# Storing the seven summed quarters of an activation where it is made, moving weight and quarter sums from GpSimd to VectorE, and chaining two of the seven products in PSUM

## The chip, the core and the metric

The kernel runs as one program on one core of a Trainium2 chip. The metric is the device time of one execution in microseconds. In what follows PE is the matmul engine, DVE is VectorE, ACT is ScalarE, POOL is GpSimd, and SP is the engine whose queue issues most transfers.

## What is computed

The reference is a two-layer encoder trunk on 1024 tokens of 1024 features, all in fp32.

```
h = x                                             # [1, 1024, 1024]
z = gelu(rmsnorm(h) @ a_w_in)                     # 1024 -> 2 * 2048
u, v = split(z); v = layernorm(v)
sv = masked(w_s) @ v + b_s                        # by groups of 256 columns, blocks of 128 tokens
h = h + (u * sv) @ a_w_out                        # 2048 -> 1024
h = h + square(relu(rmsnorm(h) @ w1[0])) @ w2[0]  # 1024 -> 4096 -> 1024
kv = shared latent keys and values of rmsnorm(h)  # computed once
h = h + attention(q(rmsnorm(h)), kv) @ w_o        # 8 heads, causal by chunks of 64
h = h + square(relu(rmsnorm(h) @ w1[1])) @ w2[1]
return rmsnorm(h)
```

Nearly all of the arithmetic is in the large products: `a_w_in`, `a_w_out`, the two `w1`, the two `w2` and `w_o`.

## The kernel before

**Operands in two parts.** Every fp32 operand of a large product is cut into a high part (a cast on ACT, L181) and a low part (the difference, a subtraction on DVE, L182). A product of 128 columns by 512 tokens over 512 features is then 4 blocks of features times 3 passes, 12 matmuls of 512 columns (`prod`, L224). Weights are split a piece of 128x512 at a time into tiles `w` (six buffers); activations are split a quarter at a time into tiles `xq`.

**Seven products instead of eight.** A large product C = A.T @ B is cut in two along columns, features and tokens. With Winograd's form of Strassen's scheme seven products of quarters replace eight:

```
S1 = A21 + A22   S2 = S1 - A11   S3 = A11 - A21   S4 = A12 - S2
T1 = B12 - B11   T2 = B22 - T1   T3 = B22 - B12   T4 = B21 - T2
P1 = A11 B11  P2 = A12 B21  P3 = S4 B22  P4 = A22 T4  P5 = S1 T1  P6 = S2 T2  P7 = S3 T3
C11 = P1 + P2                C12 = P1 + P6 + P5 + P3
C21 = P1 + P6 + P7 + P4      C22 = P1 + P6 + P7 + P5
```

A is a weight matrix, B an activation. The S are called weight sums below and the T quarter sums.

**Up-projections** (`pair_block`). The seven quarters of B stay on chip (`Resident`). A block takes 256 columns of weights (two loads `wr` of 512 KB, into four buffers), makes the four weight sums on POOL (L280, L282, L283, L293), splits seven pieces and runs 7 x 12 = 84 matmuls, then joins four outputs of 128x512 in PSUM and SBUF and hands them on. There are 8 such blocks in the u half of the first mixer (each output is also multiplied by a gate, `gate`, and POOL multiplies the weights by the norm's gain, L435) and 16 in each of the two MLPs, of which the first two run side by side (`mlp`). The v half of the first mixer has tokens as rows and its own four sums of 128x1024 on POOL, four times. The finished activation block goes to DRAM scratch (`y_d`, `g_d`; `o_d` after the attention) as four stores of 256 KB.

**Down-projections** (`down`). The activation comes back from DRAM in chunks of 1024 features: 2 chunks for `a_w_out`, 4 for each `w2`, 1 for `w_o`, 11 in all. A chunk loads four quarters of B (8 loads `yr` of 512 KB) and eight pieces of weights (`wr`), makes four quarter sums on the way (`tsum`, L212: one half of each on DVE and one on POOL, 128x1024), four weight sums for each of four column blocks m on POOL (L696 to L700), splits 7 quarters and 28 weight pieces, and runs 28 x 12 = 336 matmuls. Products 1, 6, 7 and 4 accumulate in one PSUM bank for each m (`da`); products 2, 5 and 3 have their own (`dc`). Results are added into SBUF tiles `acc` by DVE (L659): eight additions for each m.

**Order.** The program does not write out the order on the engines: a scheduler decides it for each engine from dependences and buffers. Each engine then runs its own list strictly in order, and so does each queue of transfers.

## Time and profile before

| what | value |
|---|---|
| median of 3 executions | 2450.53 us (2447.11 to 2450.75) |
| the profiled execution: span from first to last instruction | 2453.1 us |
| PE busy | 2256.7 us (92% of the span) |
| DVE busy | 1946.0 us (79%) |
| ACT busy | 1107.0 us (45%) |
| POOL busy | 954.0 us (39%) |
| moved by DMA | 257.96 MB, mean 105 GB/s |
| chain of work that ended last | PE 58%, DVE 28%, issue 6%, DMA 5%, ACT 2%, POOL 1% |

The profiled execution is one execution of its own; its span is its whole time, with nothing shown around it. Busy time is summed over instructions, and PE's matmuls overlap one another in the records, so a busy PE is not a PE that starts a matmul as often as it can.

### The profile page before, as it was taken

How to read it: one execution, taken by the hardware profiler on the slowest of the kernel's cores; microseconds unless marked ns; L12 is line 12 of the kernel's file. 1: busy time of each engine (PE TensorE's matmuls, PEld its weight loads, DVE VectorE, ACT ScalarE, POOL GpSimd, SP SyncE). 2: the span in 40 equal slices, each digit the busy share in tenths (PEclk: the TensorE clock that was granted, in tenths of full speed). 3: DMA queues.
4: the chain of work that ended last, by engine and by line, in shares of the span. 5: the costliest groups of instructions: out<-in, count | busy, mean ns of one | idle time of the engine just before them, and what ended most of it. 6: DMA issues, size and time to landing. Idle time of an engine off the chain costs nothing.

```text
span 2453.1 us, 31584 instructions
## 1 busy us (share of the span) xinstructions
PE 2256.7 (92%) x11299; PEld 1919.9 (78%) x11299; DVE 1946.0 (79%) x3040; ACT 1107.0 (45%) x2124; POOL 954.0 (39%) x616
## 2 busy tenths in 40 slices
PE   6999888898899998988989999997999999889897
PEld 6998767677678887777879898886778888678776
DVE  8647989998975558899885777779985656988997
ACT  5443334335544444433355454553654444334345
POOL 5446445643633236335431103016432333454262
PEclk8999999999999999999999999998999999899999
DMA  5224334542243335421412101033134336324302
GB/s 204 93 91 133 107 108 125 189 137 79 72 138 105 118 114 199 138 86 52 137 48 72 30 27 34 31 134 129 69 106 139 108 108 217 109 75 137 112 26 69
DMA packets 173560, 257.96 MB, mean 105 GB/s; under 512 B 13566, under 2 KB 123227, under 8 KB 173403
## 3 DMA queue, kind: packets, MB, share of 16 engines
q1 hardware_dynamic: 164016, 239.12, 30.0%
...
## 4 chain that ended last, share of the span: by engine, by line
PE 58%; DVE 28%; issue 6%; DMA 5%; ACT 2%; POOL 1%; SPq 0%; ACTq 0%; DVEq 0%; POOLq 0%
PE a L224 12%; PE da L224 11%; DVE xq L182 8%; PE dc L224 6%; DVE w L182 6%; PE c L224 6%; PE va L471 4%; PE b L224 3%; PE sc L999 3%; PE lps L837 3%; DMA V<-v_d 2%; DVE yr L212 2%; DVE acc L659 2%; PE po L1046 2%; DVE V L562 1%
## 5 line engine op out<-in xcount | busy, mean ns | idle before, releaser
L224 PE MATMUL a<-xq,w 128*128 128x512 f32 x1920 | 468.5, 396 | 27.8 <-ACT o L287 15.5
L224 PE MATMUL da<-xq,w 128*128 128x512 f32 x2112 | 489.2, 391 | 4.8 <-DVE acc L659 3.7
L224 PEld LDWEIGHTS da<-xq,w 128*128 128x128 f32 x2112 | 397.6, 189 | 88.5 <-issue 4.5
L224 PE MATMUL dc<-xq,w 128*128 128x512 f32 x1536 | 385.4, 412 | 83.5 <-DVE acc L659 49.1
L224 PEld LDWEIGHTS a<-xq,w 128*128 128x128 f32 x1920 | 364.0, 191 | 106.2 <-ACT o L287 16.5
L224 PEld LDWEIGHTS dc<-xq,w 128*128 128x128 f32 x1536 | 306.8, 201 | 157.1 <-issue 63.2
L181 ACT CAST w<-wr 128x512 fp32r<-128x512 f32 x424 | 261.5, 620 | 332.7 <-PE da L224 187.8
L182 DVE TENSOR_TENSOR w<-wr,w 128x512 fp32r<-128x512 f32 x424 | 362.3, 855 | 43.4 <-ACT w L181 43.3
L182 DVE TENSOR_TENSOR xq<-yr,xq 128x512 fp32r<-128x512 f32 x308 | 286.1, 949 | 2.3 <-ACT xq L181 2.3
L181 ACT CAST xq<-yr 128x512 fp32r<-128x512 f32 x308 | 181.5, 619 | 201.6 <-DVE yr L212 61.3
L224 PE MATMUL c<-xq,w 128*128 128x512 f32 x960 | 238.2, 398 | 11.7 <-DVE o L309 6.6
L696 POOL TENSOR_TENSOR S<-wr,wr 128x512 f32<-128x512 f32 x44 | 66.1, 1520 | 453.6 <-DMA wr<-in_mlp_w_dram 250.4
L182 DVE TENSOR_TENSOR w<-S,w 128x512 fp32r<-128x512 f32 x164 | 169.1, 1032 | 79.6 <-ACT w L181 79.4
L224 PEld LDWEIGHTS c<-xq,w 128*128 128x128 f32 x960 | 183.3, 193 | 52.3 <-issue 8.2
L280 POOL TENSOR_TENSOR S<-wr,wr 128x512 f32<-128x512 f32 x40 | 58.0, 1449 | 347.8 <-DMA wr<-in_mlp_w_dram 298.5
L181 ACT CAST w<-S 128x512 fp32r<-128x512 f32 x164 | 100.4, 619 | 134.0 <-POOL S L293 95.0
L212 POOL TENSOR_TENSOR yr<-yr,yr 128x1024 f32<-128x1024 f32 x44 | 124.1, 2820 | 21.7 <-DVE xq L182 17.9
L733 POOL TENSOR_TENSOR ssq<-ssq,sq 128x512 f32<-128x512 f32 x52 | 77.7, 1495 | 138.4 <-ACT sq L732 138.1
L784 ACT ACTIVATE o<-o 128x512 f32<-128x512 f32 x96 | 60.6, 633 | 155.8 <-DVE o L783 155.8
L659 DVE TENSOR_TENSOR acc<-da,acc 128x512 f32<-128x512 f32 x144 | 98.1, 681 | 32.8 <-PE da L224 32.6
L224 PE MATMUL b<-xq,w 128*128 128x512 f32 x480 | 120.8, 390 | 0.0
L471 PE MATMUL va<-wv,xq 128*128 128x256 f32 x768 | 103.6, 296 | 12.2 <-DVE xq L182 7.3
...
## 6 DMA issues: line engine op xcount, KB each, us to landing
wr<-in_mlp_w_dram SPq DMA_DIRECT2D x128, 512.0 KB, 5.0
yr<-y_d SPq DMA_DIRECT2D x64, 512.0 KB, 4.3
...
wr<-in_a_w_in_dram SPq DMA_DIRECT2D x32, 512.0 KB, 5.6
acc<-h_d SPq DMA_DIRECT2D x32, 512.0 KB, 7.1
...
v_d<-V SPq DMA_DIRECT2D x16, 512.0 KB, 2.6
V<-v_d SPq DMA_DIRECT2D x16, 512.0 KB, 4.9
```

The source lines that it names most:

```text
L181: nc.scalar.copy(hi, src)
L182: eng.tensor_tensor(lo, src, hi.bitcast(F32), op=ALU.subtract)
L212: e.tensor_tensor(flat(x), flat(y), flat(z), op=op)
L224: mm = nc.tensor.matmul(o, lhsT=w[:, wi, p, :], rhs=xq[p][:, xi, :], start=first and p == 0 and ip == 0, stop=p == 3 and ip == 2, skip_gro ...
L280: nc.gpsimd.tensor_tensor(S1, A21, A22, op=ALU.add)
L471: nc.tensor.matmul(oo, lhsT=xq[p][:, xi, t * P:(t + 1) * P], rhs=w[wi][:, p, :], start=first and t % 2 == 0 and p == 0 and ip == 0, stop=p ...
L659: nc.vector.tensor_tensor(x, src, x, op=ALU.add)
L696: nc.gpsimd.tensor_tensor(S1, A21, A22, op=ALU.add)
L733: nc.gpsimd.tensor_tensor(ssq[:, sl], ssq[:, sl], sq, op=ALU.add)
L784: nc.scalar.activation(y, y, AF.Square)
L837: nc.tensor.matmul(o, lhsT=X2[k % 2, j][k // 2][:, xi, tt * P:(tt + 1) * P], rhs=self.wt[k][:, wi, :], start=k == 0 and ip == 0, stop=k == ...
L999: nc.tensor.matmul(sc[c][:, 0:n], lhsT=lh, rhs=kk[c][:, part, 0:n], start=io == 0, stop=io == len(ops) - 1)
```

## The change

The activation blocks that go to DRAM are no longer the four raw quarters but the seven quarters that the products take. `Seven` takes over the scratch tensors; whoever makes a block calls `put`, which stores B11, B21 and B22 as they are and makes T1, T3, T2 and T4 (numbered by product: 5, 7, 6, 4) with one DVE subtraction of 128x512 each, as soon as their terms are there.

```diff
+    class Seven:
+        def store(self, n, f, t):
+            nc.sync.dma_start(self.d[f // 4, n - 1, f % 4 // 2][:, f % 2], t)
+        def put(self, f, i, j, t):
+            b = j ^ self.flip
+            B = self.got.setdefault(f, {})
+            B[i, b] = t
+            if (i, b) != (0, 1):
+                self.store({(0, 0): 1, (1, 0): 2, (1, 1): 3}[i, b], f, t)
+            def minus(n, x, y, into=None):
+                t = t2([P, 512], f"T{n}") if into is None else into
+                nc.vector.tensor_tensor(t, x, y, op=ALU.subtract)
+                self.store(n, f, t)
+                B[n] = t
+            if 5 not in B and (0, 0) in B and (0, 1) in B:
+                minus(5, B[0, 1], B[0, 0], B[0, 1] if 7 in B else None)
+            if 7 not in B and (0, 1) in B and (1, 1) in B:
+                minus(7, B[1, 1], B[0, 1], B[0, 1] if 5 in B else None)
+            if 6 not in B and 5 in B and 7 in B:
+                minus(6, B[1, 1], B[5], B[1, 1])
+            if 4 not in B and 6 in B and (1, 0) in B:
+                minus(4, B[1, 0], B[6])
...
-            nc.sync.dma_start(g_d[g // 4, m, j, g % 4 // 2][:, g % 2], u)
+            g_q.put(g, m, j, u)
```

`down` loads one quarter for each product, two products ahead, and makes no quarter sums. Its weight sums are on DVE. With the order 1, 2, 5, 3, 6, 7, 4 product 3 is added to product 5 in PSUM, after product 5 has been added to its other output.

```diff
-    def down(acc, y, nch, wsrc, hprev, hnext, after, order=(1, 2, 5, 6, 7, 4, 3), last=None, rpool=(None, "s"),
+    def down(acc, y, wsrc, hprev, hnext, after, order=(1, 2, 5, 3, 6, 7, 4), rpool=("s", None), last=None,
...
+            def piece(n, m):
+                A11, A21, A12, A22 = R[m, 0][:, :, lo], R[m, 0][:, :, hi], R[m, 1][:, :, lo], R[m, 1][:, :, hi]
                 if n == 5:
-                    tsum(B[0, 0], B[0, 1], B[0, 0], ALU.subtract, TENG)
...
-                        nc.gpsimd.tensor_tensor(S1, A21, A22, op=ALU.add)
-                        nc.gpsimd.tensor_tensor(A21, A11, A21, op=ALU.subtract)
-                        nc.gpsimd.tensor_tensor(A11, S1, A11, op=ALU.subtract)
-                    elif n == 3:
-                        nc.gpsimd.tensor_tensor(A12, A12, A11, op=ALU.subtract)
+                    nc.vector.tensor_tensor(S[m], A21, A22, op=ALU.add)
+                    w = w_piece(S[m])
+                    nc.vector.tensor_tensor(S[m], S[m], A11, op=ALU.subtract)
+                    return w
+                if n == 3:
+                    nc.vector.tensor_tensor(A21, A11, A21, op=ALU.subtract)
+                    nc.vector.tensor_tensor(A11, A12, S[m], op=ALU.subtract)
+                return w_piece({1: A11, 2: A12, 3: A11, 4: A22, 6: S.get(m), 7: A21}[n])
+            for at, n in enumerate(order):
+                xq = quarter(Q.pop(n))
+                if at + 2 < len(order):
+                    Q[order[at + 2]] = loadQ(order[at + 2])
...
+                    elif n == 3 and chained:
+                        o = c[m]
                     else:
-                        put(0, 1, m, o, True)
+                        o = c[m] = ps("dc")
+                    prod(o, w, xq, n in (1, 2, 5) or (n == 3 and not chained))
```

A quarter is split in two steps of 128x1024 instead of four of 128x512, the weight sums of the up-projections and of the v half move to DVE, and both halves of the resident quarter sums are on DVE.

```diff
     def quarter(raw):
-        for p in range(4):
-            x = slot([P, 2, 512], F32R, "xq")
-            split(x[:, 0], x[:, 1], raw[p // 2][:, p % 2])
-            q.append(x)
+        for r in raw:
+            x = [slot([P, 2, 512], F32R, "xq") for _ in range(2)]
+            split(flat(x[0]), flat(x[1]), flat(r))
+            q += [[part[:, p] for part in x] for p in range(2)]
...
     def pair_block(X, R, finish):
-        nc.gpsimd.tensor_tensor(S1, A21, A22, op=ALU.add)
+        nc.vector.tensor_tensor(S1, A21, A22, op=ALU.add)
...
-        nc.gpsimd.tensor_tensor(S2, S1, A11, op=ALU.subtract)
-        nc.gpsimd.tensor_tensor(A21, A11, A21, op=ALU.subtract)
+        nc.vector.tensor_tensor(S2, S1, A11, op=ALU.subtract)
+        nc.vector.tensor_tensor(A21, A11, A21, op=ALU.subtract)
...
-        nc.gpsimd.tensor_tensor(S2, A12, S2, op=ALU.subtract)
+        nc.vector.tensor_tensor(S2, A12, S2, op=ALU.subtract)
...
-                    tsum(T1, B[0, 1], B[0, 0], ALU.subtract, TENG)
+                    tsum(T1, B[0, 1], B[0, 0])
```

Besides, the first mixer takes the second half of the tokens first, `w_o` runs in the order 1, 5, 3, 6, 7, 2, 4, the stores after the attention move from ACT's queue to SP's, and comments are gone.

The lists of the engines show where the moved work stands. The first place is DVE's list in the second chunk of the first MLP's down-projection, before the change, around the quarter sums for products 6 and 7 (`yr`) and the first pieces of product 5 (`w`<-`S1`).

```order
L659 TENSOR_TENSOR acc1131_8095<-dc1293_9208,acc1131_8095 128x512
L182 TENSOR_TENSOR xq1335_9419<-yr1294_9222,xq1335_9419 128x512
L182 TENSOR_TENSOR w1328_9363<-wr1299_9232,w1328_9363 128x512
L182 TENSOR_TENSOR xq1336_9422<-yr1295_9224,xq1336_9422 128x512
L212 TENSOR_TENSOR yr1294_9222<-yr1320_9330,yr1294_9222 128x1024
L659 TENSOR_TENSOR acc1106_7990<-da1306_9246,acc1106_7990 128x512
L182 TENSOR_TENSOR w1330_9380<-wr1303_9240,w1330_9380 128x512
L212 TENSOR_TENSOR yr1300_9234<-yr1300_9234,yr1294_9222 128x1024
L659 TENSOR_TENSOR acc1106_7990<-da1307_9247,acc1106_7990 128x512
L182 TENSOR_TENSOR w1332_9397<-wr1305_9244,w1332_9397 128x512
L659 TENSOR_TENSOR acc1107_7991<-da1308_9248,acc1107_7991 128x512
L182 TENSOR_TENSOR w1339_9432<-S11338_9428,w1339_9432 128x512
```

The same list after the change, where the chunk before ends (`w`<-`wr1164` to `wr1167` are its last pieces, whose buffers `wr1264` to `wr1267` take over) and the second chunk's first weight sums stand.

```order
L182 TENSOR_TENSOR w1252_8610<-wr1164_8098,w1252_8610 128x512
L702 TENSOR_TENSOR acc1185_8191<-da1171_8109,acc1185_8191 128x512
L182 TENSOR_TENSOR xq1283_8779<-yr1262_8686,xq1282_8778 128x1024
L182 TENSOR_TENSOR w1253_8626<-wr1165_8100,w1253_8626 128x512
L182 TENSOR_TENSOR xq1285_8783<-yr1263_8688,xq1284_8782 128x1024
L702 TENSOR_TENSOR acc1182_8186<-da1168_8106,acc1182_8186 128x512
L182 TENSOR_TENSOR w1254_8642<-wr1166_8102,w1254_8642 128x512
L708 TENSOR_TENSOR S1302_8870<-wr1258_8678,wr1264_8690 128x512
L702 TENSOR_TENSOR acc1182_8186<-da1169_8107,acc1182_8186 128x512
L708 TENSOR_TENSOR S1305_8890<-wr1259_8680,wr1265_8692 128x512
L713 TENSOR_TENSOR wr1258_8678<-wr1258_8678 128x4x128
L182 TENSOR_TENSOR w1255_8658<-wr1167_8104,w1255_8658 128x512
```

The quarter sums are gone, a quarter's split is one row for two blocks, and the weight sums `S` stand between the splits and the additions, a few rows behind the split that frees the buffer of their weights.

The second place is DVE's list in the middle of an up-projection of the MLP, one block's worth of joins and splits, before the change.

```order
L309 TENSOR_TENSOR o11893_6310<-b900_6391,o11893_6310 128x512
L182 TENSOR_TENSOR w912_6463<-S1909_6444,w912_6463 128x512
L783 SCALAR_TENSOR_TENSOR o11893_6310<-o11893_6310,rbc536_4156 128x512
L182 TENSOR_TENSOR w914_6480<-S2910_6446,w914_6480 128x512
L300 TENSOR_TENSOR o12897_6345<-c889_6289,o12897_6345 128x512
L783 SCALAR_TENSOR_TENSOR o12897_6345<-o12897_6345,rbc536_4156 128x512
L182 TENSOR_TENSOR w916_6498<-S2910_6446,w916_6498 128x512
L182 TENSOR_TENSOR w917_6522<-wr904_6435,w917_6522 128x512
L304 TENSOR_TENSOR o22895_6327<-a888_6288,o22895_6327 128x512
L182 TENSOR_TENSOR w919_6544<-wr905_6437,w919_6544 128x512
L783 SCALAR_TENSOR_TENSOR o22895_6327<-o22895_6327,rbc536_4156 128x512
```

The same place after the change: `S1`<-`wr1114`, `wr1115` is the first weight sum of a block whose first product is a whole block away; `T7`, `o12` (5) and `o22` (6) are quarter sums.

```order
L182 TENSOR_TENSOR w1110_7735<-wr1095_7633,w1110_7735 128x512
L303 TENSOR_TENSOR o221083_7525<-a1076_7486,o221083_7525 128x512
L182 TENSOR_TENSOR w1111_7758<-wr1095_7633,w1111_7758 128x512
L813 SCALAR_TENSOR_TENSOR o221083_7525<-o221083_7525,rbc552_4200 128x512
L348 TENSOR_TENSOR T71088_7582<-o221083_7525,o121085_7543 128x512
L182 TENSOR_TENSOR w1118_7786<-wr1114_7780,w1118_7786 128x512
L348 TENSOR_TENSOR o121085_7543<-o121085_7543,o111081_7508 128x512
L279 TENSOR_TENSOR S11139_7938<-wr1134_7929,wr1135_7931 128x512
L348 TENSOR_TENSOR o221083_7525<-o221083_7525,o121085_7543 128x512
L813 SCALAR_TENSOR_TENSOR y1092_7624<-a1076_7486,rbc552_4200 128x512
L281 TENSOR_TENSOR S21140_7940<-S11139_7938,wr1134_7929 128x512
L282 TENSOR_TENSOR wr1134_7929<-wr1134_7929 128x4x128
```

DVE has 22 instructions a block instead of 14: four weight sums and four quarter sums more. The two weights that `S1` takes are loaded into the buffers of `wr1074` and `wr1075`, and the row `w1091` is the last to read the second of them; five rows behind `S1` stands `w1102`, the low part of the next block's piece for product 5. PE takes that piece's high part in two matmuls right behind product 1, then runs the 12 matmuls of product 6 of the block before, and only then needs the low part.

The third place is POOL's list in the u half of the first mixer, before the change: one block's work.

```order
L435 TENSOR_TENSOR wr498_3924<-wr498_3924,gT_88 128x1024
L182 TENSOR_TENSOR vh454_3660<-V424_3456,vh454_3660 128x512
L435 TENSOR_TENSOR wr499_3927<-wr499_3927,gT_88 128x1024
L280 TENSOR_TENSOR S1505_3947<-wr498_3924,wr499_3927 128x512
L282 TENSOR_TENSOR S2506_3949<-S1505_3947,wr498_3924 128x512
L283 TENSOR_TENSOR wr498_3924<-wr498_3924 128x4x128
L293 TENSOR_TENSOR S2470_3719<-wr459_3683,S2470_3719 128x512
L182 TENSOR_TENSOR vh477_3789<-V465_3706,vh477_3789 128x512
L182 TENSOR_TENSOR vh482_3827<-V465_3706,vh482_3827 128x512
L182 TENSOR_TENSOR vh488_3866<-V464_3700,vh488_3866 128x512
L182 TENSOR_TENSOR vh494_3904<-V464_3700,vh494_3904 128x512
```

After the change POOL has only the gain's multiplications and the splits `vh` there, and the sums stand on DVE, as here around the first sum of the last u block (`S1519`).

```order
L625 SCALAR_TENSOR_TENSOR sv453_3602<-svp454_3603,gT_88,B2391_3217 128x256
L625 SCALAR_TENSOR_TENSOR sv453_3602<-svp455_3610,gT_88,B2391_3217 128x256
L279 TENSOR_TENSOR S1519_3982<-wr512_3959,wr513_3962 128x512
L628 SCALAR_TENSOR_TENSOR sv448_3565<-svp449_3566,gT_88,sv448_3565 128x256
L628 SCALAR_TENSOR_TENSOR sv448_3565<-svp450_3573,gT_88,sv448_3565 128x256
L182 TENSOR_TENSOR w480_3740<-wr470_3706,w480_3740 128x512
L628 SCALAR_TENSOR_TENSOR sv453_3602<-svp454_3603,gT_88,sv453_3602 128x256
L600 TENSOR_SCALAR V514_3965<-V514_3965,mv_2148,rstd_2157 128x256 x4
L628 SCALAR_TENSOR_TENSOR sv453_3602<-svp455_3610,gT_88,sv453_3602 128x256
L281 TENSOR_TENSOR S2520_3984<-S1519_3982,wr512_3959 128x512
L282 TENSOR_TENSOR wr512_3959<-wr512_3959 128x4x128
L299 TENSOR_TENSOR o12445_3542<-c437_3486,o12445_3542 128x512
```

The sum `S1519` stands in DVE's list between the steps of the gate (`sv`), and it needs both multiplications that POOL does after the loads.

## Rows read from the trace of the kernel before

**Rows 1.** Windows: length, each engine's busy us (instructions), granted clock, DMA share, GB/s.

```profile
core 0: us, PE busy (x) PEld busy (x) DVE busy (x) ACT busy (x) POOL busy (x), PEclk, DMA share, GB/s
785.52:804.56 19.04, 19.04 (x85) 15.77 (x85) 11.32 (x14) 8.03 (x14) 5.91 (x4) 1.00 0.36 111
...
331.00:361.50 30.50, 26.89 (x130) 21.73 (x130) 26.63 (x48) 9.52 (x18) 15.46 (x12) 1.00 0.35 108
...
1069.45:1155.55 86.10, 79.07 (x337) 64.92 (x337) 77.24 (x93) 32.75 (x56) 36.98 (x20) 0.96 0.30 98
...
425.00:622.00 197.00, 176.57 (x759) 144.40 (x758) 185.32 (x231) 90.80 (x162) 101.86 (x58) 0.94 0.40 136
945.00:1298.00 353.00, 322.68 (x1366) 264.55 (x1364) 316.98 (x378) 149.78 (x261) 158.20 (x88) 0.95 0.30 100
2080.00:2420.00 340.00, 310.68 (x1340) 253.84 (x1339) 306.57 (x364) 136.02 (x235) 151.21 (x82) 0.96 0.27 89
...
1650.00:1750.00 100.00, 84.96 (x391) 70.01 (x391) 94.28 (x126) 53.83 (x107) 48.18 (x29) 0.93 0.34 122
1750.00:1816.00 66.00, 57.44 (x255) 47.26 (x254) 62.97 (x87) 39.30 (x76) 37.12 (x21) 0.92 0.26 84
```

**Rows 2.** Waits in the chunk from 1069.45 to 1155.55: total us, times, longest.

```profile
PE dc L224 <- DVE acc L659: 13.4, 2, 7.0
```

**Rows 3.** Groups of DVE in the same chunk: count, busy us, mean ns, idle before.

```profile
L182 DVE TENSOR_TENSOR xq<-yr,xq 128x512 fp32r<-128x512 f32 x29 | 27.8, 976 | 0.0
L182 DVE TENSOR_TENSOR w<-wr,w 128x512 fp32r<-128x512 f32 x24 | 21.4, 890 | 0.0
L659 DVE TENSOR_TENSOR acc<-da,acc 128x512 f32<-128x512 f32 x16 | 10.9, 683 | 4.8 <-PE da L224 4.8
L659 DVE TENSOR_TENSOR acc<-dc,acc 128x512 f32<-128x512 f32 x16 | 10.5, 674 | 0.0
L212 DVE TENSOR_TENSOR yr<-yr,yr 128x1024 f32<-128x1024 f32 x4 | 6.8, 1702 | 4.1 <-DMA yr<-y_d 4.1
L182 DVE TENSOR_TENSOR w<-S,w 128x512 fp32r<-128x512 f32 x4 | 5.6, 1412 | 0.0
```

**Rows 4.** Groups of POOL in the same chunk.

```profile
L212 POOL TENSOR_TENSOR yr<-yr,yr 128x1024 f32<-128x1024 f32 x4 | 11.1, 2770 | 1.3 <-DVE xq L182 1.2
...
L696 POOL TENSOR_TENSOR S<-wr,wr 128x512 f32<-128x512 f32 x4 | 5.6, 1423 | 42.1 <-DMA wr<-in_mlp_w_dram 42.1
```

**Rows 5.** Groups of DVE in three up-projection blocks, 785.52 to 842.64.

```profile
L783 DVE SCALAR_TENSOR_TENSOR o<-o,rbc 128x512 f32<-128x512 f32 x9 | 9.4, 1049 | 0.0
L182 DVE TENSOR_TENSOR w<-S,w 128x512 fp32r<-128x512 f32 x9 | 9.3, 1028 | 8.9 <-ACT w L181 8.9
L182 DVE TENSOR_TENSOR w<-wr,w 128x512 fp32r<-128x512 f32 x12 | 8.3, 690 | 4.4 <-ACT w L181 4.4
```

**Rows 6.** Waits in the same three blocks.

```profile
POOL S L280 <- DMA wr<-in_mlp_w_dram: 35.6, 3, 12.2
```

**Rows 7.** The page's DMA issues: count, KB each, median us from issue to landing.

```profile
wr<-in_mlp_w_dram SPq DMA_DIRECT2D x128, 512.0 KB, 5.0
yr<-y_d SPq DMA_DIRECT2D x64, 512.0 KB, 4.3
...
wr<-in_a_w_in_dram SPq DMA_DIRECT2D x32, 512.0 KB, 5.6
acc<-h_d SPq DMA_DIRECT2D x32, 512.0 KB, 7.1
```

**Rows 8.** Groups of DVE in two u blocks, 331.00 to 391.60.

```profile
L562 DVE TENSOR_SCALAR V<-V,mv,rstd 128x256 f32<-128x256 f32 x18 | 15.3, 888 | 8.4 <-DMA V<-v_d 8.4
L590 DVE TENSOR_TENSOR o<-o,sv 128x512 f32<-128x512 f32 x6 | 7.3, 1220 | 0.0
...
L586 DVE SCALAR_TENSOR_TENSOR sv<-svp,gT,B 128x256 f32<-128x256 f32 x16 | 7.0, 468 | 0.0
```

**Rows 9.** Groups of POOL in the same two u blocks.

```profile
L435 POOL TENSOR_TENSOR wr<-wr,gT 128x1024 f32<-128x1024 f32 x5 | 9.5, 1897 | 27.7 <-DMA wr<-in_a_w_in_dram 15.8 <-DVE w L182 7.7 <-DVE sv L586 4.3
...
L280 POOL TENSOR_TENSOR S<-wr,wr 128x512 f32<-128x512 f32 x3 | 4.9, 1646 | 0.2
```

More of the change, by code (lines that the diff above doesn't have):

```diff
@@ L137, in trunk_kernel @@
     xt = []
-    for t in range(4):
+    for t in range(4, NT):
         xx = slot([P, D], F32, "x")
@@ L324, in trunk_kernel, with __init__ @@
     h_d = [scratch(1, f"h_d{i}")[0] for i in range(4)]
-    y_d = [scratch(4, f"y_d{i}") for i in range(2)]
-    g_d = scratch(2, "g_d")
-    o_d = scratch(1, "o_d")
+    class Seven:
+        def __init__(self, nch, flip, name):
+            self.d = dpool.tile([nch, 7, 2, P, 2, 512], F32, name=name)
+            self.flip = flip
+            self.got = {}
+        def store(self, n, f, t):
[19 more added lines that the diff above has]
+                minus(4, B[1, 0], B[6])
+            if 4 in B:
+                del self.got[f]
+    y_q = [Seven(4, 1, f"y_d{i}") for i in range(2)]
+    g_q = Seven(2, 1, "g_d")
+    o_q = Seven(1, 1, "o_d")
     NF = DR // 2
@@ L443, in trunk_kernel @@
     xt2 = []
-    for t in range(4, NT):
+    for t in range(4):
         xx = slot([P, D], F32, "x")
@@ L564, in trunk_kernel, with gate @@
             V.append(v)
[L566 removed]
+        def gate(m, b, u, in_psum):
+            j = b ^ 1
             sl = slice(j * 512, (j + 1) * 512)
@@ L682, in down @@
                                 for ip, (wi, xi) in enumerate(PASSES):
-                                    nc.tensor.matmul(os[m][:, sl], lhsT=ws[m][:, wi, p, :], rhs=xq[p][:, xi, sl],
-                                                     start=half == 0 and p == 0 and ip == 0, stop=p == 3 and ip == 2,
-                                                     skip_group_check=True)
+                                    nc.tensor.matmul(a[m][:, sl], lhsT=ws[m][:, wi, p, :], rhs=xq[p][xi][:, sl],
+                                                     start=False, stop=p == 3 and ip == 2, skip_group_check=True)
@@ L686, in down @@
                             flush()
-                            x = acc[0, 1][m // 2][:, m % 2, sl]
+                            x = acc[1, flip][m // 2][:, m % 2, sl]
                             hn = t2([P, 256], "hn")
-                            nc.vector.tensor_tensor(hn, os[m][:, sl], x, op=ALU.add)
-                            waiting.append((0, 1, m, hn, x, half))
+                            nc.vector.tensor_tensor(hn, a[m][:, sl], x, op=ALU.add)
+                            waiting.append((1, flip, m, hn, x, half))
@@ L719, in down @@
-                    if last is not None and ch == nch - 1 and n == order[-1] and m == 1:
+                    w = piece(n, m)
+                    if n in (1, 6, 7, 4):
+                        o = a[m]
+                    elif n == 3 and chained:
+                        o = c[m]
+                    else:
+                        o = c[m] = ps("dc")
+                    prod(o, w, xq, n in (1, 2, 5) or (n == 3 and not chained))
+                    for i, b in gives[n]:
+                        put(i, b, m, o, ends[i, b] == n)
@@ L720, in down @@
+                    if last is not None and ch == nch - 1 and at == len(order) - 1 and m == 1:
                         last()
                 yield
-                if n == 1:
-                    load_rest()
+                if ch == 0 and at == 0:
+                    load_acc(1, 1)
+                    load_acc(0, 1)
+                    load_acc(1, 0)
         flush()
@@ L774, in block @@
         def block(f):
-            R = [load_rows(w1, a ^ 1, slice(f * 256, (f + 1) * 256)) for a in range(2)]
+            R = [load_rows(w1, a, slice(f * 256, (f + 1) * 256)) for a in range(2)]
             def relu2(m, b, z, in_psum):
@@ L801, in mlp @@
             run(block(f))
-        run(down(acc, y_d[l], 4, ins["mlp_w2"][l], hprev, hnext, after, last=last, halves=halves))
+        run(down(acc, y_q[l], ins["mlp_w2"][l], hprev, hnext, after, last=last, halves=halves))
     rh = cpool.tile([P, NT], F32, name="rh")
@@ L1110, in trunk_kernel @@
     fac3 = Factors(ssq3)
-    w_o = down(raw3, o_d, 1, ins["b_w_o"][0], h_d[2], h_d[3], after3, (1, 5, 2, 6, 7, 4, 3), rpool=("s", "s"))
+    w_o = down(raw3, o_q, ins["b_w_o"][0], h_d[2], h_d[3], after3, (1, 5, 3, 6, 7, 2, 4), ("s", "s"))
     for n, (h, jp) in enumerate(steps):
```

152 lines of the change are left out of this document (61 added, 91 removed).

## The prediction

> **What bounds the kernel now.** I read the windows first, then the groups and waits inside them. In a block of an up-projection PE starts a matmul every 19.04/84 = 0.2267 us and never waits, with DVE busy 11.32 us of 19.04 [rows 1]. So that stage cannot become faster, only slower. In a u block PE has 26.89 busy of 30.50 us, and DVE 26.63, nearly as much. In a chunk of a down-projection the 336 matmuls need 76.2 us at that spacing and the chunk takes 86.10: 9.9 us are PE's waits, with DVE busy 77.24 [rows 1]. The waits by name are few (13.4 us in two waits on the additions `acc` [rows 2]), so the groups of DVE say more. An addition from PSUM takes 674 to 683 ns there, while splits of the same width, which read two tiles of SBUF, take 890, 976 and 1412 [rows 3]. In the up-projection a split takes 690 and, close to POOL's sums, 1028, and a join that reads two SBUF tiles 1049 [rows 5]. So DVE's work is long where POOL works beside it: POOL is busy 36.98 us of the chunk [rows 1], 11.1 of it in halves of quarter sums at 2770 ns each [rows 4]. I read the down stages as bound by DVE, stretched by POOL.
>
> PE's waits by stage, from counts and lengths [rows 1]: down-projection of the first MLP 353.0 - 1366 x 0.2267 = 43.3; of the second 340.0 - 1340 x 0.2267 = 36.2; of the mixer 197.0 - 759 x 0.2267 = 24.9; end of the attention with `w_o` 166.0 - 646 x 0.2267 = 19.6. Together 124 us: the most that the change can take from them.
>
> **The change in a down chunk.** Gone from DVE: four halves of quarter sums (6.8 us [rows 3]) and four additions by the chain (2.7). From POOL: all of its sums. New on DVE: 16 weight sums. Counted anew at the widths seen without a neighbour: 28 splits of weights at 0.69 = 19.3, 28 additions at 0.68 = 19.0, 16 sums at 0.69 = 11.0, 14 splits of 128x1024, which no row shows, between 2 x 0.69 = 1.38 and 2 x 0.976 = 1.95 each [rows 3, 5]; I take the lower end, since the 0.976 was measured beside POOL, so 19.3. The sum is 68.7 us (76.7 by the upper end) of 76.2. DVE stops being the longest, with 7 us to spare. It does get a wait: a sum needs weights that land 5.0 us after their buffer is free [rows 7], and it stands five to nine rows (3.4 to 6.2 us) behind the split that frees it, so DVE stands still some 1.5 us four times, 6 us, with splits for five pieces of 2.72 us ahead of PE as cover. POOL had that wait for nothing (42.1 us of idle time a chunk [rows 4]). Loads rise from 8 to 11 MB a chunk (14 instead of 8 tiles of a quarter), of which 16 engines are now 0.30 busy [rows 1], and a quarter (4.3 us [rows 7]) is asked for two products, 21.8 us, ahead. I leave 1.2 us of the 9.9 in each chunk, and 3 us at a stage's start, where sums of the first pieces wait for loads. Taken back: 36 of 43.3, 28 of 36.2, 17 of 24.9, 11 of 19.6, in all 92 us (bounds 124 and nothing).
>
> **Up-projections, 28 blocks.** DVE gets four weight and four quarter sums: 22 x 0.69 = 15.2 us of 19.04, which fits. The question is the order. The weights of the first sum are asked for when the last split that reads their buffer ends. That split follows the join of product 7, 24 matmuls (5.4 us) ahead of the end of product 4; with join and split of 0.69 each the load starts 4.1 us ahead of that end. It lands 5.0 us later [rows 7], at +0.9. The sum and five more rows end at +5.0, and PE needs the low part of product 5 after 12 + 2 + 12 matmuls, at +5.9. So 0.9 us remain, and each us of landing above 5.9 costs 28 us in all. POOL sat in this wait 35.6 us of three blocks [rows 6], harmlessly. The three added stores a block raise traffic from 111 to about 152 GB/s. I take +4 us (0 to +60).
>
> **u half, 8 blocks.** DVE has 26.63 of 30.50 us [rows 1]. Added: eight sums, 5.5 us. POOL loses four sums of some 1.3 to 1.65 us, 5.5 of its 15.46 [rows 1, 9], about 36%. The stretch by POOL now is about (1.22 - 0.69) x 4 = 2.1 (the gate's four products) and (0.89 - 0.47) x 9 = 3.8 us a block, taking the 468 ns of a step from PSUM as the bare price of the 256-wide `V` [rows 8]; 36% of it is 2.1. That makes 30.0. The first sum also waits for a load (5.6 us [rows 7]) and then for POOL's gain step (1.9 us [rows 9]), with some rows of `sv` between as cover; I take 2 us. So 32.0 instead of 30.5, +1.5 a block, +12 (-8, if the load is covered and the stretch goes more than in proportion, to +48, if POOL's steps stretch DVE as before and the wait is whole).
>
> **The rest.** v half: 16 sums of 128x1024 move to DVE, about 1.38 each, 22 us, hidden where DVE idles; +3 (-4 to +8). Starts of the MLPs, where both halves of the resident sums now stand on DVE: +5 (0 to +10). Attention: its quarter sums hold small buffers longer, and its stores queue on SP behind loads; +3 (0 to +15). SP's queue else: an added store waits for its tile, and the loads behind it need a later split anyway; 0.
>
> **Sum.** -92 + 4 + 12 + 3 + 5 + 3 = -65 on the profiled 2453.1, so 2388. That execution lies 2.6 us above the median of 2450.53; against the median it is 2386.
>
> **The Trainium skill** (Perfetto Trace Analysis, Optimizing Scalar/DVE Operations) says that work may be taken off a saturated DVE to ScalarE or even GpSimd, with the caveat that DVE and GpSimd share a read port, so that moving work between those two might not help. The change goes against the first half, since it loads the busier engine further; the traces bear out the caveat (690 against 1028 ns for the same split). By the first half the time would be that of the third rival below, by the caveat that of the sum.
>
> **The rivals.**
> 1. *Half the gain.* The chunk is tied to its transfers and to the wait in DVE's list more than I think: eight weights and fourteen quarter tiles come in bunches, and `acc` loads already take 7.1 us [rows 7]. Then -46 + 27 = -19: 2432. For it: 42.1 us of POOL's idle time is weights coming late [rows 4]; against it: DVE at 77.24 of 86.10 explains the chunk alone.
> 2. *Slower by the wait in DVE's list.* If weights land later than 5.9 us in the up-projections, PE waits in each of 28 blocks. With -92 + 23 elsewhere the kernel is slower than before by more than the bound from 5.9 + 74/28 = 8.5 us on; at 9.0 us: -69 + 87 = +18, 2468. For it: nothing hides the wait now; against: 5.0 us is the median.
> 3. *DVE stays stretched.* If splits keep 0.97 us and the sums take 1.41 without POOL's sums beside them, a chunk has 27.0 + 19.0 + 22.6 + 27.3 = 96 us of DVE, 10 more than now: 11 x 10 + 27, 2587. Against: POOL is nearly empty in these chunks.
> 4. *The down stages don't move* (transfers bound them): +27, 2478.
> 5. *No costs outside.* The waits are covered and DVE in the u half gains what POOL gives up: -92 + 4, 2362.
>
> **How the numbers follow.** Chances: the forecast 0.57 (2360 to 2412), half gain 0.18, slower by the wait 0.07, stretched 0.03, not moved 0.03, no costs 0.12. A measurement of this kernel tells 0.2%, 5 us, from no change. Faster: 0.57 + 0.12 + most of 0.18 and a little of the second = 0.83; same 0.05, between half gain and loss; slower 0.12. The range of 8 in 10 reaches from a little beyond rival 5 to a little beyond rival 1, 2340 to 2440; it leaves out the cases above.
>
> **What would show it.** Chunks of 76.5 to 79 us with DVE below 72 and splits near 0.69 us confirm the main term; splits still near 0.9 or chunks above 82 refute it. Up blocks of 19.04 to 19.3 us confirm the second; a wait of PE on DVE's split of `S1` in each block, with DVE waiting for `wr`, refutes it. u blocks near 32 us confirm the third. The prediction is wrong above all if landings grow by 1 to 3 us with 66 MB more traffic, or if the u half falls behind by DVE alone.

## The result and the profile after

The changed kernel takes 2393.89 us (median of 4 runs, 2388.44 to 2401.05) against 2450.64 before: ratio 0.9769, 95% interval 0.9748 to 0.9789. The forecast was 2386. The profiled execution took 2388.44 us with a span of 2386.7.

The page's totals first; POOL is all but idle, and DVE is no busier than before although it does POOL's sums.

```profile
span 2386.7 us, 31463 instructions
PE 2234.5 (94%) x11299; PEld 1898.9 (80%) x11299; DVE 1882.9 (79%) x3288; ACT 1096.1 (46%) x1920; POOL 247.5 (10%) x208
```

The windows that answer to [rows 1] are a steady chunk of the first MLP's down-projection, a steady up block and a piece of the u half, in the columns of that group.

```profile
1021.20:1097.40 76.20, 76.20 (x338) 63.10 (x337) 61.63 (x87) 31.65 (x43) 0.00 (x0) 1.00 0.46 152
...
823.32:843.70 20.38, 19.11 (x84) 15.50 (x83) 13.82 (x22) 8.02 (x14) 0.00 (x0) 1.00 0.44 142
331.00:361.50 30.50, 25.55 (x119) 21.45 (x119) 28.44 (x52) 10.43 (x19) 9.99 (x6) 0.94 0.39 122
```

The chunk takes exactly its 336 matmuls, 76.20 us. The up block, which had no wait before, takes 20.38 instead of 19.04. The groups of DVE in the chunk, to set beside [rows 3]:

```profile
L182 DVE TENSOR_TENSOR xq<-yr,xq 128x1024 fp32r<-128x1024 f32 x15 | 18.3, 1222 | 3.5 <-PE da L225 2.4 <-ACT xq L181 1.0
L182 DVE TENSOR_TENSOR w<-wr,w 128x512 fp32r<-128x512 f32 x20 | 13.7, 686 | 0.0
L702 DVE TENSOR_TENSOR acc<-da,acc 128x512 f32<-128x512 f32 x16 | 11.0, 686 | 3.7 <-PE da L225 3.6
...
L182 DVE TENSOR_TENSOR w<-S,w 128x512 fp32r<-128x512 f32 x8 | 5.5, 688 | 0.0
...
L708 DVE TENSOR_TENSOR S<-wr,wr 128x512 f32<-128x512 f32 x4 | 2.8, 690 | 1.2 <-DMA wr<-in_mlp_w_dram 1.2
```

A split of weights is down from 890 ns to 686, those of sums from 1412 to 688, an addition from PSUM is where it was (683 then), and DVE's wait for weights, now on L708, is 1.2 us a chunk.

Lengths of the stages, each from the start of its first product in PE's timeline to that of the next (us; the third column is experiment e8, below):

| stage | before | changed | e8: only the sums moved |
|---|---|---|---|
| up to the end of the u half | 443.8 | 445.2 | 420.1 |
| down-projection of the mixer | 180.7 | 159.4 | 161.9 |
| up-projection, first MLP | 313.1 | 328.3 | 311.9 |
| down-projection, first MLP | 359.9 | 316.1 | 320.1 |
| latents | 90.9 | 90.9 | 90.9 |
| attention and `w_o` | 374.4 | 372.4 | 375.1 |
| up-projection, second MLP | 309.7 | 332.0 | 309.3 |
| down-projection, second MLP, and the end | 380.6 | 342.3 | 347.8 |

The three down stages give 103 us, the two up stages take 37 back, and the rest is even.

Where the up block loses its 1.3 us is in the timeline of the changed kernel (start, length, engine, operation, and in brackets the idle time ahead and what ended it). `y` is the join of product 4, and L286 is ACT's copy of product 1 out of bank `a`, on which product 6 is then accumulated.

```profile
808.83 5.60 PE L225 MATMUL a<-xq,w 128*128 128x512 f32 x24
...
810.34 0.68 DVE L348 TENSOR_TENSOR o<-o,o 128x512 f32<-128x512 f32 x1
...
812.78 0.69 DVE L279 TENSOR_TENSOR S<-wr,wr 128x512 f32<-128x512 f32 x1 [1.76 <-DMA wr<-in_mlp_w_dram]
813.44 0.69 DVE L348 TENSOR_TENSOR o<-o,o 128x512 f32<-128x512 f32 x1
814.05 0.68 DVE L813 SCALAR_TENSOR_TENSOR y<-a,rbc 128x512 f32<-128x512 f32 x1
814.27 0.61 PE L225 MATMUL c<-xq,w 128*128 128x512 f32 x2
...
814.77 0.63 ACT L814 ACTIVATE y<-y 128x512 f32<-128x512 f32 x1 [2.39 <-DVE y L813]
...
815.30 0.57 ACT L286 COPY o<-a 128x512 f32<-128x512 f32 x1
...
815.92 3.04 PE L225 MATMUL a<-xq,w 128*128 128x512 f32 x12 [1.04 <-ACT o L286]
```

Product 4 ends about 811.6 (the first 12 of the 24 matmuls from 808.83), but `y` starts at 814.05, two rows behind the first weight sum, which waits for its load; the quarter sum for product 6 stands between them. ACT squares `y` and only then makes the copy, and PE waits 1.04 us before product 6. The copied product 1 isn't the one that ends at 814.3, which belongs to the block after: PE runs each product 1 about a block ahead. The end of the stage shows it, where no further block follows:

```profile
910.92 5.60 PE L225 MATMUL a<-xq,w 128*128 128x512 f32 x24
...
936.47 0.58 ACT L286 COPY o<-a 128x512 f32<-128x512 f32 x1
...
939.48 2.88 PE L225 MATMUL a<-xq,w 128*128 128x512 f32 x12
```

The last product 1 ends at 916.4 (the second 12 of the 24), its copy starts 20 us later, and the last product 6 follows at 939.48. So product 6 doesn't wait for a product; it waits for the place of the copy in ACT's list, behind the square of `y`.

### The profile page after: what moved, and what is told of

It reads as the page before. It is cut to its first block, busy times and chain, and to the rows that moved or that the text cites. A ratio compares the mean times of both kernels' runs of the same rounds, so it can differ in the third digit from the quotient of the medians.

```text
span 2386.7 us, 31463 instructions
## 1 busy us (share of the span) xinstructions
PE 2234.5 (94%) x11299; PEld 1898.9 (80%) x11299; DVE 1882.9 (79%) x3288; ACT 1096.1 (46%) x1920; POOL 247.5 (10%) x208
## 5 line engine op out<-in xcount | busy, mean ns | idle before, releaser
L181 ACT CAST w<-wr 128x512 fp32r<-128x512 f32 x380 | 235.4, 621 | 382.1 <-PE da L225 156.1
L225 PE MATMUL dc<-xq,w 128*128 128x512 f32 x1584 | 364.7, 389 | 1.3 <-ACT xq L181 1.3
L182 DVE TENSOR_TENSOR w<-wr,w 128x512 fp32r<-128x512 f32 x380 | 275.8, 728 | 30.7 <-ACT w L181 28.9
L181 ACT CAST w<-S 128x512 fp32r<-128x512 f32 x208 | 128.4, 622 | 182.7 <-PE dc L225 80.4
L182 DVE TENSOR_TENSOR xq<-yr,xq 128x1024 fp32r<-128x1024 f32 x154 | 188.0, 1223 | 14.4 <-PE da L225 7.2
L181 ACT CAST xq<-yr 128x1024 fp32r<-128x1024 f32 x154 | 160.8, 1051 | 63.7 <-PE dc L225 20.1
L182 DVE TENSOR_TENSOR w<-S,w 128x512 fp32r<-128x512 f32 x208 | 143.6, 695 | 23.4 <-ACT w L181 23.4
L702 DVE TENSOR_TENSOR acc<-dc,acc 128x512 f32<-128x512 f32 x116 | 79.5, 686 | 51.3 <-PE dc L225 51.3
L225 PEld LDWEIGHTS b<-xq,w 128*128 128x128 f32 x480 | 94.8, 201 | 22.8 <-issue 2.1
L509 PEld LDWEIGHTS va<-wv,xq 128*128 128x128 f32 x768 | 95.4, 195 | 15.1 <-ACT xr L452 10.7
```

The lines of the kernel that those rows point to most:

```text
L181: nc.scalar.copy(hi, src)
L182: eng.tensor_tensor(lo, src, hi.bitcast(F32), op=ALU.subtract)
L225: mm = nc.tensor.matmul(o, lhsT=w[:, wi, p, :], rhs=xq[p][xi], start=first and p == 0 and ip == 0, stop=p == 3 and ip == 2, skip_group_che ...
L509: nc.tensor.matmul(oo, lhsT=xq[p][xi][:, t * P:(t + 1) * P], rhs=w[wi][:, p, :], start=first and t % 2 == 0 and p == 0 and ip == 0, stop=p ...
L702: nc.vector.tensor_tensor(x, src, x, op=ALU.add)
```

## The experiments

Four questions: is it this wait that lengthens the up blocks (e1, e2, e3, e5, e6, e12)? Was it POOL beside DVE, or DVE's count of work, that bound the chunks (e4)? Which half of the change brings the gain (e8, e11)? And what holds the attention (e9)? With e10 and e13 I only looked for a better version. Ratios are to the kernel before on the same chip, where it took 2452 to 2455 us.

**e1_up_pool.** `pair_block` takes the sums' engine; POOL for the MLPs.

```diff
-        nc.vector.tensor_tensor(S1, A21, A22, op=ALU.add)
+        seng.tensor_tensor(S1, A21, A22, op=ALU.add)
...
-            return pair_block(X, R, relu2)
+            return pair_block(X, R, relu2, nc.gpsimd)
```

> The changed kernel with the four weight sums of the MLPs' up-projection blocks back on POOL (nothing else). Theory W (the wait in DVE's list): in the changed kernel the first sum of a block waits up to 2 us for its weights in DVE's list, the join of product 4 and its square come late, and PE waits before product 6; an up block takes 20.4 instead of 19.04 us. With the sums on POOL the wait stands there: blocks of 19.0 to 19.4 us, the whole 28 x 1.1 to 1.35 = 30 to 38 us faster than the changed kernel, 2356 to 2366 us. Rival L (the load): the longer block comes from the quarter sums, the added stores and fewer free small buffers, all of which stay; the time stays at 2394 within 5 us, or rises, since POOL's sums stretch DVE's quarter sums.

Measured: 2413.21 us, 0.9843 (0.9825 to 0.9861), slower than the changed kernel. Blocks take 20.8 to 21.0 us (from one first sum on POOL to the next). Two waits in a stretch of eight blocks:

```profile
DVE o L348 <- DMA y_d<-o: 18.3, 7, 2.8
...
PE c L225 <- DVE w L182: 13.4, 8, 1.9
```

DVE now waits for a store: the quarter sum for product 6 is written over the raw quarter (`o22`) whose store must have read it. In the changed kernel this wait lies inside that of S1. And POOL's sums stretch DVE's work again: the quarter sum for product 4 takes 1657 ns on average, 684 in the changed kernel. PE now waits for the low part of product 5, the row that the prediction had watched. Theory W as I had put it, one wait, fell.

**e2_up_first_pool.** As e1, with S1 alone on POOL.

> The changed kernel with only the first weight sum (S1) of the MLPs' up-projection blocks on POOL; the other three stay on DVE. Theory W: only the instruction that waits for the weights matters, so nearly all of the gain of all four comes back: blocks of 19.0 to 19.5 us, 2358 to 2370 us. Rival L: 2394 within 5 us. Between them (DVE's number of instructions matters too): blocks near 19.9, about 2380.

Measured: 2426.16 us, 0.9889 (0.9871 to 0.9908); blocks of 21.1 us. DVE waits for the store here as well (2.7 us a block), and in seven blocks of the two stages S2 on DVE waits for POOL's S1 (14.4 us in all). Against both readings.

**e3_up_slots.** Half of the weights of an up block goes to the larger buffers, so that loads start earlier.

```diff
-            R = [load_rows(w1, a, slice(f * 256, (f + 1) * 256)) for a in range(2)]
+            R = [load_rows(w1, a, slice(f * 256, (f + 1) * 256), ("s", None)[a]) for a in range(2)]
```

> The changed kernel with all sums on DVE, but half of each up block's weights loaded into the 31 larger buffers instead of the four weight buffers, so that loads can start a block or more earlier. Theory W: the wait of the first sum on DVE goes without POOL's help; blocks of 19.0 to 19.4 us, 2358 to 2368 us. Rival L: 2394 within 5 us. If the buffers that it takes are missed at the stages' starts, some 5 to 15 us come on top in either case.

Measured: 2398.36 us, 0.9783 (0.9766 to 0.9799), the same as the changed kernel. The wait of S1 is gone in its timeline, and the other stands in its place:

```profile
820.14 0.69 DVE L348 TENSOR_TENSOR o<-o,o 128x512 f32<-128x512 f32 x1 [2.30 <-DMA y_d<-o]
820.75 0.68 DVE L813 SCALAR_TENSOR_TENSOR y<-a,rbc 128x512 f32<-128x512 f32 x1
...
822.06 0.69 DVE L279 TENSOR_TENSOR S<-wr,wr 128x512 f32<-128x512 f32 x1
```

Steady blocks take 19.75 to 20.0 us, and the start of the stage loses what they gain.

**e4_down_pool.** The down-projections' weight sums on POOL, all else as changed.

```diff
-                    nc.vector.tensor_tensor(S[m], A21, A22, op=ALU.add)
+                    nc.gpsimd.tensor_tensor(S[m], A21, A22, op=ALU.add)
...
-                    nc.vector.tensor_tensor(A21, A11, A21, op=ALU.subtract)
+                    nc.gpsimd.tensor_tensor(A21, A11, A21, op=ALU.subtract)
```

> The changed kernel with the weight sums of the down-projections back on POOL. In the changed kernel a steady chunk takes 76.20 us, PE without a wait and DVE busy 61.6. Theory S (DVE has slack in a chunk once quarter sums and a quarter of the additions are gone): POOL's 16 sums of 1.3 to 1.7 us beside DVE stretch splits of two SBUF tiles from 0.69 to 0.75-0.9, DVE busy 55 to 65 us, chunk 76.2 to 77.5, in all 0 to +15 us against the changed kernel. Rival C (it was POOL's sums beside DVE that bound the chunk): chunk 79 us or more, +30 us or more.

Measured: 2396.76 us, 0.9772 (0.9757 to 0.9786), the same. The chunk as a window, and its groups on DVE and POOL:

```profile
1021.20:1097.40 76.20, 76.20 (x338) 63.10 (x337) 59.48 (x71) 31.54 (x44) 27.83 (x16) 1.00 0.46 152
...
L182 DVE TENSOR_TENSOR w<-wr,w 128x512 fp32r<-128x512 f32 x20 | 17.3, 864 | 0.0
L702 DVE TENSOR_TENSOR acc<-da,acc 128x512 f32<-128x512 f32 x16 | 10.9, 684 | 5.7 <-PE da L225 5.6
...
L714 POOL TENSOR_TENSOR wr<-wr,S 128x512 f32<-128x512 f32 x4 | 7.2, 1811 | 0.3
```

This is the cleanest measure of one engine beside the other, since nothing else differs: with POOL's sums a split from SBUF takes 864 ns instead of 686, an addition from PSUM 684 instead of 686. Taking 16 sums off DVE saves it only 2 us of busy time (59.48 against 61.63). And the chunk stays at 76.20: with the quarter sums gone, DVE has room for either. Theory S held.

**e5_t6_slots and e6_t6_only.** The sum for product 6 in a buffer of its own, with 30 larger and 9 small buffers (31 and 7); e5 with the loads of e3, e6 without.

```diff
-                minus(6, B[1, 1], B[5], B[1, 1])
+                minus(6, B[1, 1], B[5])
```

> As e3_up_slots, and the quarter sum for product 6 is written to a small buffer of its own instead of over the raw quarter whose store it must wait for (30 larger and 9 small buffers instead of 31 and 7, which pays for it). Theory W2 (two waits stand one behind the other in DVE's list: S1's for its weights, and the sum's for the store of the tile that it overwrites; taking away one leaves the other): both are gone, steady up blocks take 19.04 to 19.2 us, 20 us or more below e3_up_slots, 2365 to 2380 us. Rival L (DVE's eight added instructions make the block longer whatever they wait for): blocks stay at 19.7 or more, 2393 to 2403 us.

> The changed kernel with the sum for product 6 in a small buffer of its own and 30 larger and 9 small buffers, the weights' loads as in the changed kernel. Theory W2: S1's wait of some 2 us remains and decides, as the store's wait lies inside it in the changed kernel; blocks of 20.2 to 20.4 us, 2388 to 2402 us. If the store's wait alone were the cause: blocks of 19.1 us, about 2360. If nine small buffers alone help the blocks, the same.

Measured: 2425.12 us, 0.9880 (0.9865 to 0.9894), and 2426.36, 0.9882 (0.9867 to 0.9897), both slower. In e6, without the store's wait, steady up blocks take 20.2 to 20.7 us, as forecast for S1's wait alone. In e5 they take 19.48 us, from 20.38 in the changed kernel and 19.75 to 20.0 in e3. But e5 did not take both waits out, as was expected of it: the store's is gone, and S1 still waits for weights, 13.2 us in eight blocks, now ahead of the join of product 7:

```profile
857.25 0.69 DVE L279 TENSOR_TENSOR S<-wr,wr 128x512 f32<-128x512 f32 x1 [1.66 <-DMA wr<-in_mlp_w_dram]
...
865.05 2.17 PEld L225 LDWEIGHTS c<-xq,w 128*128 128x128 f32 x10 [0.53 <-DVE w L182]
```

The second line is where the 0.4 us above 19.04 lie: in each block PE's weight loads wait 0.4 to 0.6 us for the low part of product 5, which stands behind `y` in DVE's list. One large buffer less costs more elsewhere: from the first u product to the first of the down-projection e6 takes 278.1 us, the changed kernel 247.1. The totals decide nothing. The blocks agree with two waits in series, of which either alone costs the larger part; no run of the changed kernel has neither.

**e8_before_dve.** The kernel before, with only the engine changed for the sums of the down-projections, of `pair_block` and for the POOL halves of the quarter sums (the v half's four sums stayed on POOL).

```diff
-    TENG = (nc.vector, nc.gpsimd)
+    TENG = (nc.vector, nc.vector)
...
-        nc.gpsimd.tensor_tensor(S1, A21, A22, op=ALU.add)
+        nc.vector.tensor_tensor(S1, A21, A22, op=ALU.add)
...
-                        nc.gpsimd.tensor_tensor(S1, A21, A22, op=ALU.add)
+                        nc.vector.tensor_tensor(S1, A21, A22, op=ALU.add)
```

> The kernel before with all weight sums and both halves of the quarter sums on DVE (four raw quarters in DRAM, eight additions, splits of 128x512 and the order of products as before). Tells the move to DVE from the rest. Theory S: what stretched DVE's splits was POOL beside it, so splits fall from 0.89-0.98 to about 0.69-0.75; DVE's bare work a chunk is then 32 additions at 0.68, 56 splits at 0.69, 8 halves of sums at 1.3 and 16 sums at 0.69, 82 us, so chunks of 82 to 85 us (85.5 before) and DVE above 95% busy; the storing of seven quarters is what brings a chunk down to 76. Rival M (the move alone brings the gain): chunks of 76 to 79 us. Rival 3 of the prediction (splits stay stretched): chunks of 93 us or more. Time 2430 to 2480 by theory S, with the up blocks longer by S1's wait.

Measured: 2339.01 us, 0.9529 (0.9507 to 0.9550): twice the gain of the whole change. Its up block and its chunk as windows, and groups of DVE in the chunk:

```profile
785.00:804.04 19.04, 19.04 (x86) 15.77 (x85) 11.71 (x18) 8.05 (x15) 0.00 (x0) 1.00 0.37 111
1005.00:1081.20 76.20, 76.20 (x338) 63.08 (x337) 72.32 (x113) 33.45 (x57) 0.00 (x0) 1.00 0.34 111
...
L182 DVE TENSOR_TENSOR xq<-yr,xq 128x512 fp32r<-128x512 f32 x28 | 18.6, 677 | 0.0
L182 DVE TENSOR_TENSOR w<-wr,w 128x512 fp32r<-128x512 f32 x24 | 16.3, 678 | 0.0
L212 DVE TENSOR_TENSOR yr<-yr,yr 128x1024 f32<-128x1024 f32 x9 | 10.9, 1213 | 1.0 <-DMA yr<-y_d 1.0
```

Rival M was right, and theory S too pessimistic. DVE does all of a chunk's work, 113 instructions instead of 93, in 72.32 us instead of 77.24 [rows 1], since each step is shorter: 976 to 677 and 890 to 678 ns [rows 3], and a half of a quarter sum 1702 to 1213. My 82 us counted busy lengths that overlap by some 0.08 us from one instruction to the next (timelines show starts 0.60 us apart for steps of 0.69). The up blocks keep 19.04 us although S1 waits for its weights on DVE here too.

**e11_down_dve.** As e8, with `pair_block` as before (its sums on POOL).

> As e8_before_dve, but the up-projection blocks' sums (of the u half and of both MLPs) stay on POOL; on DVE are only the down-projections' weight sums and all quarter sums. If the down stages alone bring e8's gain there: they keep chunks of 76.2 us, and the u half returns from 217.9 us towards the 232.9 of before, since POOL's sums stretch DVE's splits there: 2350 to 2362 us. If the move of the up blocks' sums brings nothing in the u half: 2339 within 5 us.

Measured: 2365.41 us, 0.9648 (0.9630 to 0.9665). This is a little above the 2350 to 2362 us of the first reading. Of e8's 116 us, 87 come from the down-projections' and quarter sums and 29 from the up blocks'. The u half takes 233.2 us with POOL's sums, as before (232.9), and 217.9 in e8, which is half of the 29.

**e12_sums_only.** As e8, with the four quarter sums of the changed kernel made for every block of the MLPs and not stored or used.

```diff
                 nc.sync.dma_start(y_d[l][f // 4, m, j, f % 4 // 2][:, f % 2], y)
+                Y[f, m, b] = y
+                if len([1 for k in Y if k[0] == f]) == 3:
+                    T = Y[f, "T"] = t2([P, 512], "T")
+                    nc.vector.tensor_tensor(T, Y[f, 1, 1], Y[f, 0, 1], op=ALU.subtract)
+                    nc.vector.tensor_tensor(T, Y[f, 0, 1], Y[f, 0, 0], op=ALU.subtract)
+                    nc.vector.tensor_tensor(Y[f, 1, 1], Y[f, 1, 1], T, op=ALU.subtract)
+                if (m, b) == (1, 0):
+                    nc.vector.tensor_tensor(Y[f, "T"], y, Y[f, 1, 1], op=ALU.subtract)
```

> As e8_before_dve, and each finished block of the MLPs' up-projections makes the four quarter sums of the changed kernel on DVE, the one for product 6 over the raw quarter whose store it must wait for, but stores none of them; the down-projections don't use them. Doubles the suspected cost without the transfers. Theory W2 (the sums and their wait in DVE's list make the up blocks longer): the MLPs' up stages, 311.9 and 309.3 us in e8 and 328.4 and 332.0 in the changed kernel, take 322 to 334 us, in all 2360 to 2385 us. Rival T (the stores and the traffic do it): up stages stay within 3 us of e8, 2339 to 2346 us.

Measured: 2368.54 us, 0.9658 (0.9641 to 0.9675), but not by way of the steady blocks: the up stages take 320.5 and 319.4 us (e8: 311.9 and 309.3), between the two readings, and most of it is lost at their starts. A steady block as a window, and DVE's timeline around S1 in it:

```profile
801.58:820.62 19.04, 19.04 (x86) 15.77 (x84) 14.31 (x23) 8.14 (x15) 0.00 (x0) 1.00 0.36 110
...
804.50 0.69 DVE L784 SCALAR_TENSOR_TENSOR y<-a,rbc 128x512 f32<-128x512 f32 x1 [0.44 <-PE a L224]
805.15 0.69 DVE L182 TENSOR_TENSOR w<-wr,w 128x512 fp32r<-128x512 f32 x1
807.31 0.69 DVE L280 TENSOR_TENSOR S<-wr,wr 128x512 f32<-128x512 f32 x1 [1.47 <-DMA wr<-in_mlp_w_dram]
```

DVE has the 22 instructions of the changed kernel and S1's wait of about the same length, and PE waits for nothing. So neither DVE's count nor a wait as such makes the block longer. Here `y` stands ahead of S1; in the changed kernel it stands behind. That what stands behind the wait decides is read from the two timelines and not shown alone: in e12 no sum is stored either, ACT copies product 1 ahead of the square of `y`, and PE takes the products in another order.

**e9_att_actq.** The stores after the attention on ACT's queue (`self.q` is `nc.scalar` for `o_d`).

```diff
-            nc.sync.dma_start(self.d[f // 4, n - 1, f % 4 // 2][:, f % 2], t)
+            self.q.dma_start(self.d[f // 4, n - 1, f % 4 // 2][:, f % 2], t)
```

> The changed kernel with the stores after the attention on ACT's queue again, instead of on SP's behind and ahead of the loads. The attention takes 287.8 us in the changed kernel and 275.9 before. Theory Q (stores that wait for a head's result hold up the next heads' weights on SP's queue): 276 to 280 us, 8 to 12 us faster than the changed kernel, 2382 to 2388. Rival B (the small buffers that the quarter sums hold longer delay those loads and copies): within 3 us of the changed kernel.

Measured: 2392.20 us, 0.9745 (0.9731 to 0.9760), the same as the changed kernel within the intervals; the attention takes 290 us by the start of its first and of `w_o`'s first product. Theory Q fell. Attention and `w_o` together are even in all three columns of the table, so much of what looked like a cost is where one stage's first product falls.

**e10_dve_wide and e13_dve_wide_v.** e8 with `quarter` as in the changed kernel (steps of 128x1024), and e10 with the v half's sums on DVE too.

> As e8_before_dve (sums on DVE, four raw quarters in DRAM), with a quarter's split in two steps of 128x1024 as in the changed kernel. e8 takes 2339 us, its steady chunks 76.2 us with DVE busy 72.4. Theory: a step of 128x1024 takes 1.22 us against two of 0.68, so DVE falls to some 70 us a chunk, and the starts of the stages, where PE waits for splits, gain a little: 2328 to 2339 us. Rival: coarser steps let PE wait longer for a stage's first quarter, 2340 to 2350.

> As e10_dve_wide, with the v half's four weight sums on DVE too, as in the changed kernel: a candidate for the best version. The time up to the end of the u half is 420.1 us in e8. If POOL's sums of 128x1024 stretch DVE there: 5 to 10 us less than e10; if DVE has no time left between the v half's splits: 0 to 5 us more.

Measured: 2334.32 us, 0.9519 (0.9504 to 0.9534), and 2332.80, 0.9514 (0.9499 to 0.9529). Both lie within the uncertainty of e8 and of each other. By their medians they are the best versions; e13 takes 0.9514/0.9769 = 0.974 of the changed kernel's time.

## Why the prediction was right, and where it was not

The total was right and so was the main mechanism: DVE bound the down stages, stretched by POOL. That the total came so close, -66 us between the two profiled executions (-57 between the medians) where -65 was forecast, is luck. The sizes were wrong and cancelled: the down stages gave 22 us more than forecast and the first mixer's two halves 14 more, the up stages cost 28 more, and the attention with `w_o` gave 6 less. And the working did not see that half of the change alone brings more than the whole.

*Down stages, -81 for three of them (and -11 for `w_o`).* Measured -103: chunks of 76.20 us, no wait of PE left where I had left 1.2 us a chunk, DVE's wait for weights 1.2 us where I had 6, and DVE busy 61.6 us where I had 68.7. A split of 128x1024 takes 1.22 us, below the lower end of my bound, and lengths overlap. `w_o` and the attention together gave 2 us of the 8 forecast.

*Up-projections, +4, and the MLPs' starts, +5.* Measured +37. This is the step that failed: "So 0.9 us remain". The load and S1 came when I had reckoned (S1 starts 1.2 us behind the end of product 4, reckoned 0.9), and the landings kept their median, as the page of the changed kernel shows, so the second rival's late landing never came:

```profile
wr<-in_mlp_w_dram SPq DMA_DIRECT2D x128, 512.0 KB, 5.0
```

But I followed only the low part of product 5 behind the waiting sum. PE needs it later than I had reckoned, behind the 12 matmuls of product 3 as well (the 22 of bank `c` from 818.80 start with them, since the join of product 3 starts at 821.9). The row two behind the sum, `y`, starts 2.4 us late, and it holds ACT's square, ACT's copy of product 1 and so product 6. (The rows shown ahead of the prediction have the sum as `S11139`, from `wr1134`; the names in the text beside them, `wr1074` to `w1102` and `S1` from `wr1114`, are those of the block before.) The store's wait, of the sum written over a raw quarter, was not in my working at all: I had set the stores at nothing beyond traffic. e1 and e3 show that it takes the place of S1's.

*u half and v half, +12 and +3.* Measured +1.4 up to the end of the u half. Cut at the first u product, the u half took 247.1 us against 232.9, +14.2 and near the forecast; what comes ahead of it took 198.1 against 210.9, -12.8 where I had +3, so that this term had the wrong sign. In e13, where only the v half's sums move, the first u product comes at 198.1 us against 204.6 in e10. The two edits in the u half go opposite ways: moving the sums alone brings 23.7 us up to its end (e8), so the lifting of POOL's stretch is worth more than the four sums, where I had it worth less; the rest of the change takes 25 back. The step on `V`, which normalises a tile of v for the gate, shows the stretch over the u half, before, changed and in e8:

```profile
L562 DVE TENSOR_SCALAR V<-V,mv,rstd 128x256 f32<-128x256 f32 x64 | 49.4, 821 | 20.0 <-DMA V<-v_d 20.0
```

```profile
L600 DVE TENSOR_SCALAR V<-V,mv,rstd 128x256 f32<-128x256 f32 x64 | 30.9, 539 | 0.0
```

```profile
L562 DVE TENSOR_SCALAR V<-V,mv,rstd 128x256 f32<-128x256 f32 x64 | 30.7, 530 | 4.1 <-DMA V<-v_d 3.7 <-POOL vh L182 0.5
```

POOL lost 36% of its work there by my count, and I took 36% of the stretch away; of the 821 ns nearly all that lies above 530 went, with 16 to 20 us of DVE's waiting for `V`. The whole half as a window, of the changed kernel and of e8:

```profile
198.10:445.20 247.10, 208.13 (x945) 172.86 (x944) 234.04 (x431) 88.58 (x159) 74.61 (x44) 0.91 0.48 156
```

```profile
202.23:420.09 217.86, 199.54 (x958) 165.07 (x956) 211.57 (x400) 88.20 (x164) 83.42 (x44) 0.96 0.45 146
```

In both DVE is busy 95 to 97% of the time, and PE 84 and 92%, so I read DVE as what bounds the u half. The 22 us more of DVE, 31 instructions, are most of the 29 us more of the stage: the quarter sums there fall on the engine that has no room. PE's granted clock differs too, 0.91 and 0.96; what that costs here was not separated.

*Which half.* I priced the change as a whole, and "DVE stops being the longest" can be had in more than one way. In the down stages the two are substitutes: with seven quarters stored, POOL may keep the sums (e4, 76.20 us a chunk); with the sums on DVE, four raw quarters do (e8, 76.20). By the table the changed kernel is only some 12 us ahead of e8 over three down stages, and 39 us behind it in the up stages and 25 up to the end of the u half. Of the 39, the quarter sums alone, unstored, make up 19 (e12). Between e10 and the changed kernel lie the seven stored quarters, the chain of product 3 to product 5, the orders of products, tokens and buffers, together +55 us by the two spans (2331.9 and 2386.7); I did not take these apart further. That the chain costs or gains is not shown.

*The third rival* (DVE stays stretched) fell with 686 ns. By the Trainium skill (Perfetto Trace Analysis, Optimizing Scalar/DVE Operations) its caveat held, that offloading between DVE and GpSimd might not help since they share a read port, and its advice to offload from a saturated DVE did not: the opposite move gave 4.7% here. The Trainium skill (SBUF — State Buffer, Who interferes with whom) states that a DVE instruction with two SBUF inputs contends with a GpSimd instruction that reads SBUF, and that one with at most one SBUF input, outside the modes that use two ports, does not. The run e4 agrees, with 686 to 864 ns for the split and 686 to 684 for the addition from PSUM.

*Left open.* What decides that `y` stands behind S1 in the changed kernel and ahead of it in e12 is the scheduler's order; whether the three more stores a block, by holding small buffers longer, led it there was not tried. Nor was `y` put ahead of S1 in the changed kernel with all else as it is, which would show the cause of the longer blocks alone. What e12 loses at the stages' starts was not traced either.
